# A hybrid SSD and retention decoder layer: three short per-head vectors loaded as rows and spread over the partitions by a matmul

## Chip, cores and metric

The kernel runs on one core of one Trainium2 chip. The metric is the device time of one execution in microseconds (us).

## The reference

One decoder layer on x (1 x 1024 x 1024, float32). RMSNorm, one combined input projection, and its columns go to two groups of heads that are computed side by side: a Mamba-2 state-space group (SSD: 16 heads, chunks of 128 tokens) and a retention group (8 heads). Their outputs are concatenated, projected and added to x; a SwiGLU feed-forward block and a final RMSNorm follow. Three vectors of 16 numbers, one number for each SSD head, matter here:

```python
dt = softplus(dt_raw + dt_bias)                     # dt_bias: 16
a = -exp(a_log)                                     # a_log:   16
a_cs = cumsum(dt * a)                               # within a chunk
...
y = y_diag + y_off + x_c * d_skip[head]             # d_skip:  16
```

## The kernel before

Tokens are worked on in two halves of 512 (h = 0, 1), each of four tiles of 128 tokens. Every float32 matmul of a projection is made of three matmuls on operands split into a rounded part and a rest: `divide(k)` of a block takes one 128-row slice of weights (tile `wr`, 256 KB, five buffers), ScalarE writes the rounded part (line 248) and VectorE the rest (line 249). Below, `wr` slices are counted from 0. A global list of steps, one for each slice of each block, fixes the order on TensorE; `advance` issues weight loads up to three steps ahead of the divided one on SyncE's queue (line 238), and functions hung on a step with `at` run behind it.

The start is written out by hand. SyncE's queue gets the first token tile of x (512 KB), weight slices 0 to 3, the second tile of x, and then slice 4 and on. ScalarE's queue gets the 128x128 identity (`kc`) and `norm1_w`. GpSimd's queue gets the other norm and convolution vectors as rows (`rows`, line 105), which TensorE later turns into columns (`make_cols`). Nine matmuls on a tile of ones go first on TensorE. `turn(0)` then transposes the first token tile; for each of its eight 128-column pieces, ScalarE and VectorE write the split, scaled `h` (lines 1171, 1172), with the weights' divides between them. The first block (`v0`) walks its steps by token tile: steps 0 and 1 are token tile 0, steps 2 and 3 token tile 1, and so on; each step is 12 matmuls of 512 columns. Behind `turn(0)` stand the loads of token tiles 2 and 3, and `load_small()`.

`load_small` issues the load of the large table `kcB` on SyncE and four loads on GpSimd's queue. Two of them fill `dcol` (128 x 8): the lower 64 partitions get the 8 even entries of `d_skip` each, the upper 64 the 8 odd ones, so source and destination pieces are single float32 numbers, two apart in memory. The other two spread `dt_bias` and `a_log` over all 128 partitions of `hb` (128 x 32), 64 bytes to each. Behind step 12 `use_small` turns `a_log` into -exp(a_log) in place (ScalarE line 115, VectorE line 116), and the second `make_cols` does the `rows` (TensorE line 135, ScalarE line 137). `hb` is first read in `dt_stage` of the first half, `dcol` when SSD pieces are put together (line 661).

PSUM has two rings of banks, L (5) for the blocks and M (3) for the rest.

Of the kernel before, what the change touches and what calls it, by code (L numbers as in the profile page):

```python
# [12 lines left out]
AF = mybir.ActivationFunctionType  # L13
# [4 lines left out]
P = 128  # L18
# [6 lines left out]
SH, SP_, SG = 16, 64, 2  # L25
# [40 lines left out]
def block_kernel(ctx: ExitStack, tc: tile.TileContext, x, norm1_w, w_in, conv_w, conv_b,  # L66
                 dt_bias, a_log, d_skip, ssd_norm_w, ret_norm_w, w_out, norm2_w, w_gate,
                 w_up, w_down, final_norm_w, consts, out):
    nc = tc.nc
# [9 lines left out]
    def T(shape, tag, dt=F32, bufs=1):  # L79
        uid[0] += 1  # L80
        return sb.tile(list(shape), dt, tag=tag, name=f"{tag}_{uid[0]}", bufs=bufs)

    def bank(tag):
        uid[0] += 1
        return psum.tile([P, 512], F32, tag=tag, name=f"{tag}_{uid[0]}", bufs={"L": 5, "M": 3}[tag])
# [5 lines left out]
    act = nc.scalar.activation  # L91
# [17 lines left out]
    hb = T([P, 2 * SH], "hb")  # L109
    dcol = T([P, 8], "dcol")  # L110
    ones = T([P, P], "ones")
    nc.vector.memset(ones, 1.0)

    def use_small():
        act(hb[:, SH:2 * SH], hb[:, SH:2 * SH], AF.Exp)
        ts(hb[:, SH:2 * SH], hb[:, SH:2 * SH], -1.0, None, op0=ALU.mult)

    def load_small():
        nc.sync.dma_start(kc, consts[:, P:])
        for j in range(2):  # L120
            nc.gpsimd.dma_start(dcol[64 * j:64 * j + 64, :],
                                d_skip[0].rearrange("(k j) -> j k", j=2)[j]
                                .partition_broadcast(64))
        for j, src in enumerate((dt_bias, a_log)):
            nc.gpsimd.dma_start(hb[:, j * SH:(j + 1) * SH], src[0].partition_broadcast(P))

    dtb = hb[:, 0:SH]
    aneg = hb[:, SH:2 * SH]
# [30 lines left out]
    def mm(o, a, b, start=True, stop=True, **kw):  # L159
        tc.keep_in_program_order(nc.tensor.matmul(o, a, b, start=start, stop=stop, **kw))  # L160
# [1018 lines left out]
    b = bank("M")  # L1179
# [10 lines left out]
    for t in (2, 3):  # L1190
        first_load(t)
    load_small()
    at(ROWS, first_rows)

    def late_small():

        with tc.issue_after(newest["act"]), tc.issue_after(newest["dve"]):
            use_small()
            make_cols(False)
# [78 lines left out]
```

## Time and profile before

| | |
|---|---|
| median of 3 runs (lowest, highest) | 1528.23 us (1526.89, 1529.42) |
| profiled execution, its own time | 1528.46 us |
| its span, first to last instruction | 1526.7 us |
| TensorE matmul busy | 1496.4 us, 98% of the span |
| VectorE, ScalarE, GpSimd busy | 1018.6, 625.2, 33.2 us |
| DMA moved | 208.68 MB |

The span is the time from the first to the last instruction; 1.8 us of the execution's own time lie outside it. Busy shares are averages over the span. Engines are PE (TensorE matmul), PEld (its weight load), DVE (VectorE), ACT (ScalarE), POOL (GpSimd), SP (SyncE); a q behind a name is the engine's queue of DMA issues. An arrow `out<-in` names the tiles, and L248 is line 248 of the kernel.

### The profile page before, as it was taken

What the parts mean: (1) busy time and instruction counts of PE and PEld (TensorE: products, weight loads), DVE (VectorE), ACT (ScalarE), POOL (GpSimd) and SP (SyncE); (2) the same over time, 40 slices, a digit from 0 to 9 for tenths busy, and PEclk for the clock granted to TensorE, in tenths of its full rate; (3) what the DMA queues carried; (4) which work ended last, traced back from release to release, by engine and by line L of the source; (5) the groups of instructions that cost most, each with busy time, mean ns of one, the idle gap of its engine ahead of it and who ended that gap; (6) DMA issues with size and microseconds to landing.
All of it is one profiled execution on the core that took longest, in us unless ns stands there. A gap on an engine that the chain in (4) does not pass through costs nothing.

```text
span 1526.7 us, 20790 instructions
## 1 busy us (share of the span) xinstructions
PE 1496.4 (98%) x7408; PEld 1222.3 (80%) x7408; DVE 1018.6 (67%) x2175; ACT 625.2 (41%) x1219; POOL 33.2 (2%) x67
## 2 busy tenths in 40 slices
PE   6999999999999999999999899999999999999997
PEld 5888878887889878878887688888888887788886
DVE  4587788767688896578746976666666665346345
ACT  5344457444354655333444522222222234344232
POOL 1011000000000000000000000000000000000000
PEclk8999999999999999999999999999999999999999
DMA  7433466473425567645533332222222238455331
GB/s 195 137 92 98 116 203 190 121 242 105 130 77 148 167 204 248 214 146 175 187 118 97 97 111 78 81 83 83 76 83 83 83 105 293 133 176 188 126 112 68
DMA packets 139369, 208.68 MB, mean 137 GB/s; under 512 B 11172, under 2 KB 69376, under 8 KB 139264
## 3 DMA queue, kind: packets, MB, share of 16 engines
q1 hardware_dynamic: 138096, 205.90, 43.6%
q0 software_dynamic: 432, 0.59, 0.6%
q8 instruction: 58, 0.95, 0.3%
q10 hardware_dynamic: 736, 0.86, 0.2%
q14 instruction: 47, 0.39, 0.1%
HBM read 166.34 MB, written 40.96 MB: 136 GB/s over the span
## 4 chain that ended last, share of the span: by engine, by line
PE 92%; DMA 4%; DVE 2%; ACT 1%; issue 1%; SPq 0%; ACTq 0%; DVEq 0%
PE L L160 74%; PE M L160 16%; PE M L163 2%; DMA m<-aD 1%; DMA wr<-in_w_in_dram 1%; DMA wr<-in_w_down_dram 1%; DVE m L196 0%; DMA x<-in_w_gate_dram 0%; DMA kc<-in_consts_dram 0%; DMA ktok<-aD 0%; ACT m L195 0%; DMA m<-mixD 0%; DVE wp L249 0%; DVE u L1019 0%; ACT wp L248 0%
## 5 line engine op out<-in xcount | busy, mean ns | idle before, releaser
L249 DVE TENSOR_TENSOR wp<-wr,wp 128x512 fp32r<-128x512 f32 (+2 forms) x328 | 217.7, 665 | 224.3 <-ACT wp L248 223.1
L160 PE MATMUL L<-wp,m 128*128 128x512 f32 x1512 | 357.3, 395 | 1.5 <-DVE wp L249 0.9
L248 ACT ACTIVATE wp<-wr 128x512 fp32r<-128x512 f32 (+2 forms) x328 | 199.6, 610 | 361.8 <-PE L L160 294.9
L160 PEld LDWEIGHTS L<-wp,m 128*128 128x128 f32 x1512 | 282.0, 188 | 68.7 <-DVE wp L249 2.4
L160 PE MATMUL L<-wp,h 128*128 128x512 f32 (+2 forms) x1248 | 260.0, 365 | 0.0
L160 PEld LDWEIGHTS L<-wp,h 128*128 128x128 f32 x1248 | 215.4, 188 | 30.6 <-issue 5.1
L160 PE MATMUL L<-h,wp 128*128 128x512 f32 x972 | 234.1, 398 | 0.7 <-ACT ktok L166 0.7
L160 PEld LDWEIGHTS L<-h,wp 128*128 128x128 f32 x972 | 180.6, 188 | 44.5 <-ACT ktok L166 1.1
L160 PE MATMUL L<-m,x 128*128 128x512 f32 x336 | 82.7, 395 | 1.6 <-ACT x L195 1.2
L160 PE MATMUL L<-h,x 128*128 128x512 f32 x336 | 83.3, 396 | 0.7 <-ACT ktok L166 0.7
L160 PE MATMUL L<-m,wp 128*128 128x512 f32 x312 | 77.1, 395 | 0.0
L160 PEld LDWEIGHTS L<-m,x 128*128 128x128 f32 x336 | 62.9, 188 | 17.2 <-ACT x L195 1.6
L160 PEld LDWEIGHTS L<-h,x 128*128 128x128 f32 x336 | 62.9, 188 | 16.3 <-ACT ktok L166 1.1
L160 PEld LDWEIGHTS L<-m,wp 128*128 128x128 f32 x312 | 58.5, 187 | 14.4
L195 ACT ACTIVATE wp<-wr 128x512 fp32r<-128x512 f32 x46 | 29.0, 630 | 66.6 <-DVE wr L948 57.5
L195 ACT ACTIVATE x<-x 128x512 fp32r<-128x512 f32 x40 | 24.9, 623 | 72.5 <-PE M L160 32.4
L389 DVE SCALAR_TENSOR_TENSOR m<-m,cols,m 128x512 f32<-128x512 f32 x72 | 52.1, 745 | 3.6 <-ACT m L387 3.4
L160 PE MATMUL M<-m,wp 128*128 128x512 f32 x216 | 53.4, 395 | 0.0
L160 PEld LDWEIGHTS M<-m,wp 128*128 128x128 f32 x216 | 40.5, 188 | 9.9
L160 PE MATMUL M<-m,x 128*128 128x512 f32 x192 | 47.1, 394 | 0.0
L196 DVE TENSOR_TENSOR m<-m 128x512 fp32r<-128x512 f32 x32 | 21.8, 690 | 35.5 <-ACT m L195 35.5
L160 PE MATMUL M<-h,x 128*128 128x512 f32 x180 | 44.5, 395 | 0.0
(280 smaller groups left out, 1952.4 us busy)
## 6 DMA issues: line engine op xcount, KB each, us to landing
wr<-in_w_in_dram SPq DMA_DIRECT2D x144, 256.0 KB, 2.8
wr<-in_w_down_dram SPq DMA_DIRECT2D x88, 256.0 KB, 2.9
wr<-in_w_out_dram SPq DMA_DIRECT2D x64, 256.0 KB, 2.9
aD<-u SPq DMA_DIRECT2D x44, 256.0 KB, 2.0
x<-in_w_gate_dram SPq DMA_DIRECT2D x22, 512.0 KB, 3.9
x<-in_w_up_dram SPq DMA_DIRECT2D x22, 512.0 KB, 3.9
x<-in_x_dram SPq DMA_DIRECT2D x16, 512.0 KB, 4.1
m<-rD SPq DMA_DIRECT2D x16, 512.0 KB, 4.1
```

The lines of the kernel that those rows point to most:

```text
L160: tc.keep_in_program_order(nc.tensor.matmul(o, a, b, start=start, stop=stop, **kw))
L163: tc.keep_in_program_order(nc.tensor.transpose(o, a, ident))
L195: a = act(pair[:, 0], src, AF.Copy).ins
L196: d = tt(pair[:, 1], src, pair[:, 0].bitcast(F32), op=ALU.subtract).ins
L248: newest["act"] = act(pair[:, 0, :n], raw[:, :n], AF.Copy).ins
L249: newest["dve"] = tt(pair[:, 1, :n], raw[:, :n], pair[:, 0, :n].bitcast(F32), op=ALU.subtract).ins
L389: stt(dst, u[:, q:q + TH], w[q], dst, op0=ALU.mult, op1=ALU.add)
```

## The change

The three vectors are loaded as rows of 64 bytes into one partition (a tile of 1 x 48 that shares the buffer `at` with a later tile), from GpSimd's queue right behind the `rows` loads. Behind step 12 one matmul of a row of ones (128 wide) against this row puts all 48 numbers into all 128 partitions of an M bank, and ScalarE copies them from there: `dt_bias` as it is, `a_log` through Exp, and `d_skip` twice, its even entries to the lower 64 partitions of `dcol` and the odd ones to the upper 64. The four spreading loads go.

```diff
+    small = T([1, 3 * SH], "at")
+    for j, src in enumerate((dt_bias, a_log, d_skip)):
+        nc.gpsimd.dma_start(small[:, j * SH:(j + 1) * SH], src)
+
     def use_small():
-        act(hb[:, SH:2 * SH], hb[:, SH:2 * SH], AF.Exp)
+
+        b = bank("M")
+        mm(b[:, :3 * SH], ones[:1, :], small)
+        act(hb[:, :SH], b[:, :SH], AF.Copy)
+        act(hb[:, SH:2 * SH], b[:, SH:2 * SH], AF.Exp)
         ts(hb[:, SH:2 * SH], hb[:, SH:2 * SH], -1.0, None, op0=ALU.mult)
+        d = b[:, 2 * SH:3 * SH].rearrange("p (k j) -> p j k", j=2)
+        for j in range(2):
+            act(dcol[64 * j:64 * j + 64, :], d[64 * j:64 * j + 64, j, :], AF.Copy)
 
     def load_small():
         nc.sync.dma_start(kc, consts[:, P:])
-        for j in range(2):
-            nc.gpsimd.dma_start(dcol[64 * j:64 * j + 64, :],
-                                d_skip[0].rearrange("(k j) -> j k", j=2)[j]
-                                .partition_broadcast(64))
-        for j, src in enumerate((dt_bias, a_log)):
-            nc.gpsimd.dma_start(hb[:, j * SH:(j + 1) * SH], src[0].partition_broadcast(P))
```

## Rows read from the trace of the kernel before

**Rows 1.** The page: busy times, and the span in 40 slices (tenths).

```profile
PE 1496.4 (98%) x7408; PEld 1222.3 (80%) x7408; DVE 1018.6 (67%) x2175; ACT 625.2 (41%) x1219; POOL 33.2 (2%) x67
...
PE   6999999999999999999999899999999999999997
```

**Rows 2.** The chain that ended last, 0 to 120 us: start, us, what.

```profile
0.74 4.60 DMA kc<-in_consts_dram
...
5.36 14.11 DMA wr<-in_w_in_dram
...
19.50 0.63 ACT m L248
...
23.79 6.41 PE L L160 x24
```

**Rows 3.** Waits, 0 to 30 us: total, times, longest.

```profile
PE L L160 <- ACT h L1171: 10.1, 2, 9.9
ACT m L248 <- DMA wr<-in_w_in_dram: 10.0, 1, 10.0
```

**Rows 4.** Timeline of SyncE's queue: start, duration of the issue.

```profile
7.38 0.33 SPq L238 DMA_DIRECT2D wr<-in_w_in_dram  x1
...
8.24 3.73 SPq L238 DMA_DIRECT2D wr<-in_w_in_dram  x1
...
12.06 2.91 SPq L238 DMA_DIRECT2D wr<-in_w_in_dram  x1
...
15.06 1.62 SPq L238 DMA_DIRECT2D wr<-in_w_in_dram  x1
...
16.73 0.62 SPq L1134 DMA_DIRECT2D x<-in_x_dram  x1
```

**Rows 5.** DMA by queue, 0 to 7.8 us.

```profile
DMA packets 1114, 2.01 MB, mean 258 GB/s; under 512 B 209, under 2 KB 395, under 8 KB 1114
...
q0 software_dynamic: 155, 0.04, 2.5%
```

**Rows 6.** DMA by queue, 7.8 to 16.8 us.

```profile
DMA packets 197, 0.33 MB, mean 37 GB/s; under 512 B 81, under 2 KB 89, under 8 KB 197
...
q0 software_dynamic: 68, 0.01, 80.8%
```

**Rows 7.** DMA by queue, 16.8 to 30 us.

```profile
q0 software_dynamic: 65, 0.01, 0.5%
```

**Rows 8.** DMA issues of the first 20 us: KB, median us from issue to landing.

```profile
dcol<-in_d_skip_dram POOLq DMA_DIRECT2D x2, 2.0 KB, 11.6
...
hb<-in_dt_bias_dram POOLq DMA_DIRECT2D x1, 8.0 KB, 13.7
```

**Rows 9.** DMA issues from 60 to 1520 us, the same columns.

```profile
wr<-in_w_in_dram SPq DMA_DIRECT2D x129, 256.0 KB, 2.7
```

**Rows 10.** By stretch: busy times, granted clock, DMA share, GB/s.

```profile
6.00:7.50 1.50, 1.42 (x10) 0.96 (x9) 0.84 (x2) 1.50 (x5) 0.66 (x2) 1.00 1.07 393
...
12.00:19.50 7.50, 0.00 (x0) 0.00 (x0) 0.00 (x0) 0.00 (x1) 0.00 (x0) 0.50 0.84 125
19.50:25.70 6.20, 5.27 (x17) 4.37 (x18) 4.24 (x10) 5.46 (x16) 0.00 (x0) 0.50 0.95 342
25.70:30.20 4.50, 4.50 (x22) 3.69 (x21) 2.36 (x7) 4.02 (x14) 0.00 (x0) 1.00 0.79 265
```

**Rows 11.** Timeline of TensorE, 8 to 58 us.

```profile
8.34 2.15 PE L160 MATMUL L<-m,h 128*128 128x512 f32 x6 [0.17 <-ACT h L1171]
...
21.88 1.91 PE L163 MATMUL M<-kc,x 128*128 128x128 f32 x8
23.44 6.76 PE L160 MATMUL L<-m,h 128*128 128x512 f32 x24
30.04 1.03 PE L163 MATMUL M<-kc,x 128*128 128x128 f32 x8
30.82 5.72 PE L160 MATMUL L<-m,h 128*128 128x512 f32 x24
...
53.03 0.24 PE L135 MATMUL M<-kc,rows 84*128 84x84 f32 x1
```

**Rows 12.** Timeline of ScalarE and VectorE, 7 to 54 us.

```profile
7.53 1.28 DVE L249 TENSOR_TENSOR m<-wr,m 128x512 fp32r<-128x512 f32 x2
...
8.79 0.68 ACT L1171 ACTIVATE h<-M,cols 128x128 fp32r<-128x128 f32 x2
...
28.83 0.35 DVE L1172 SCALAR_TENSOR_TENSOR h<-M,cols,h 128x128 fp32r<-128x128 f32 x1 [0.52 <-ACT h L1171]
...
52.04 0.20 ACT L115 ACTIVATE hb<-hb 128x16 f32<-128x16 f32 x1
...
53.23 0.43 ACT L248 ACTIVATE wp<-wr 128x272 fp32r<-128x272 f32 x1 [0.98 <-PE L L160]
```

## The prediction

> **What bounds the kernel now.** I read the page first: TensorE is busy 98% of the span, and its digit is 9 in nearly every slice but the first, which has a 6 [rows 1]. So a change pays only where TensorE stands still or where it adds to TensorE's own queue, and the first slice is the one place near this change. The chain of work that ended last says what stands in that slice: one weight load, issued at 5.36 us, carries 14.11 us of the chain, and behind it the chain is matmuls nearly without a break [rows 2]. The waits of the first 30 us give the same gap from two sides: ScalarE's divide waits 10.0 us in one piece for a weight slice, and TensorE waits 9.9 us in one piece for the `h` that ScalarE writes behind that divide [rows 3]. ScalarE had ended its work before it at 8.79 + 0.68 = 9.47 us [rows 12] and began the divide at 19.50.
>
> Why does 256 KB take 14 us, when the same load takes 2.7 us later in the kernel [rows 9]? It isn't late issue: slice 4 went out at 5.36 [rows 2], and on SyncE's queue slice 5 at 7.38, in 0.33 us. The issues behind them swell to 3.73, 2.91 and 1.62 us [rows 4]: they are held back by engines that take nothing. The DMA view by queue shows by what. From 7.8 to 16.8 us only 0.33 MB moved, 37 GB/s, where 393 GB/s was reached just before [rows 6, 10]. In those 9 us the software queue, GpSimd's, moved 0.01 MB in 68 packets and held 80.8% of all 16 DMA engines: 0.808 x 9.0 x 16 = 116 us of engine time [rows 6]. The software loads in flight then are those of `dcol` and `hb`, which land 11.6 and 13.7 us after issue [rows 8]. Of the two I blame `dcol`: 2 x 64 x 8 = 1024 separate 4-byte numbers, 116 us / 1024 = 113 ns each. In the stretch behind, 65 software packets take 0.005 x 13.2 x 16 = 1.1 us together, 16 ns each [rows 7], so packets in whole 64-byte or longer pieces are cheap. The sum doesn't hang on this split, since all four loads go.
>
> **The change part by part.**
>
> *Four spreading loads removed.* The 116 us of engine time go, 7.3 us on each of the 16 engines. What is late next? At 7.8 us, 2.01 MB had moved [rows 5], of about 2.1 MB asked for ahead of slice 4 (two token tiles of 0.52 MB, four slices of 0.26 MB, the identity). The rest and slice 4 itself are some 0.4 MB, 1.0 us at 393 GB/s: the last byte passes at about 8.8 us. Landing adds something; 2.7 us from issue to landing, less 0.7 us of transfer, bounds it by 2.0 us [rows 9]. So slice 4 lands between 8.8 and 10.8 us. ScalarE isn't free before 9.47. I take a divide at 9.7 in place of 19.50, nearer the early end, since its descriptors wait ready and part of that 2.0 us is issue: 9.8 us off, bounds 8.6 and 10.0.
>
> Do the next slices keep up? Slice 5, issued at 7.38, lands at about 7.38 + 2.7 = 10.1; slice 6, issued at 8.24, at 10.9; slice 7 waits for its buffer until VectorE ends at 7.53 + 1.28 = 8.81 and lands at about 11.5 [rows 4, 9, 12]. ScalarE asks for them one divide and one `h` piece apart, about 0.77 us: 10.5, 11.25 and 12.0. Each is in time by 0.3 to 0.5 us. The third tile of x, out at 16.73 [rows 4], can go at about 10 and is wanted by transposes at 30.04 - 9.8 = 20.2 [rows 11]. Hence nothing of the 9.8 us is given back there.
>
> *TensorE's clock.* It was granted 0.50 (1.2 GHz) in 12.0 to 19.5 and 19.5 to 25.7 us, and 1.00 (2.4 GHz) from then on [rows 10]; before it fell the engine had stood still since 8.34 + 2.15 = 10.5 us [rows 11]. With the gap down to a few tenths I expect 1.00 throughout. Eight transposes took 1.91 us at the low level and 1.03 at the high, 24 matmuls 6.76 against 5.72 [rows 11]: at most 0.88 + 1.04 = 1.9 us. At least nothing, because the `h` pieces of token tile 1 end at 28.83 + 0.35 = 29.2 us [rows 12], only 1.0 us before the matmuls that use them end, so TensorE can't run far ahead. ScalarE itself would shift some tenths, because its first piece of that tile waits for these transposes. I take 0.8.
>
> The Trainium skill, TensorE: Matmul & The Clock Gate, section HAM oscillation, says that a wait for a DMA makes the gate throttle the array and that the matmuls behind it start cold. The trace agrees (0.50 behind the 9.9 us wait). By it the 0.8 us are earned when the wait goes; without it they are not, and the sum would be 1519.1.
>
> *Three row loads added.* Each is one run of 64 bytes. At the cheap end they cost 16 ns a packet [rows 7]. At the dear end, 113 ns for each of 48 numbers all on one engine, 5.4 us; were `hb` and not `dcol` the culprit, 116 us / 256 runs = 0.45 us a run, 1.4 us for three. I take nothing: the run is contiguous, nearest to the cheap rows. They are issued on GpSimd's queue behind the `rows` loads, where nothing else waits but the memset of `halo`, which is read much later.
>
> *Matmul and copies behind step 12.* TensorE gains one matmul of 48 columns; the nearest row is the 84-column one beside it, 0.24 us [rows 11]. Between 0.1 and 0.5, I take 0.3; it is on the path. ScalarE gains three copies of about 0.20 us [rows 12], and its Exp, which ran free at 52.04, now waits for that matmul, with the next divide queued behind it. That divide stood idle 0.98 us for a buffer before it began [rows 12], since ScalarE works ahead of TensorE there: the three copies and the wait hide in it. Without that cover they would cost some 0.8 + 0.6 us once. The M ring is claimed once more; its banks were read out long before.
>
> *Sum*, against the profiled execution's own 1528.46 us (0.2 above the median shown): 1528.46 - 9.8 - 0.8 + 0.3 = 1518.2.
>
> **The rivals.**
>
> *The clock falls all the same.* While token tile 0 is worked on, ScalarE sets the pace and TensorE runs in pieces; the clock fell at 12.0 us behind just that stage. If it falls at that time again and stays low for the 6 us or more that it was low under work [rows 10], it meets some 3 us of matmuls that ran at full clock before, and these take 1.5 us more at half: instead of 0.8 won, 1.5 lost, 1518.2 + 0.8 + 1.5 = 1520.5. Against it: before, a stop of 10 us stood there.
>
> *Loads come just too late.* The slices pace ScalarE because fixed landing times, hidden before by the long stop, now show: slice 4 at 10.8, and some tenths for each of the next. Then 7.5 us are won and the time is 1520.5 to 1521. Against it: the margins worked out above.
>
> *Rows read number by number on one engine.* 5.4 us on one engine, and every weight slice needs all 16: 1518.2 + 5.4 = 1523.6. Against it: runs of 64 bytes were cheap.
>
> *The stop isn't the small loads'.* The loads removed are 20 KB. If the engines were waiting for something else (memory, or the depth of SyncE's own ring), slice 4 stays late: 1528.46 + 0.3 = 1528.8, no change. Against it: 80.8% of the engines held by that queue alone. The Trainium skill, DMA: Bandwidth & Descriptors, section Anatomy of one DMA, prices such a load at a fixed 2 us plus its bytes, which would make the four loads harmless; the trace disagrees (11.6 us to land, and the engines held).
>
> *Slower.* At step 12 ScalarE holds the next divides while it waits for the new matmul, and TensorE starves. TensorE has three slices in hand there, 12 matmuls of 272 columns each, some 1.5 us a slice; ScalarE would have to stand for 4.6 us plus the 10 us won plus 3 us. Its waits there are 1 us long, and the row loads will have landed 20 us before. Time if so: from 1531.6.
>
> **How the numbers follow.** Two executions of this kernel differ by about 0.1 to 0.2%, so 0.2% (3.1 us) is the bound of what counts as a change. Forecast 0.62; clock 0.14; late loads 0.10; number by number 0.05; not the small loads 0.05; slower 0.04. The forecast's own bounds are 1528.46 - 10.0 - 1.9 + 0.1 = 1516.7 and 1528.46 - 8.6 + 0.5 = 1520.4. The range takes these in, and the clock and the late loads with them, with half a microsecond and more for the spread between executions: 1516.0 to 1521.5. Faster 0.62 + 0.14 + 0.10 + 0.05 = 0.91, same 0.05, slower 0.04.
>
> **What would show it.** Right: ScalarE's wait for a weight slice falls from 10.0 us to under 1; the issues of slices 6 to 8 take about 0.3 to 0.4 us each; the software queue's share from 7.8 to 16.8 us falls from 80.8% to about nothing; the granted clock shows no 0.50 between 12 and 26 us; line 135's neighbour has a new matmul of 0.1 to 0.5 us, and TensorE has no gap there. Wrong: a wait of several us for `wr` or `h` within the first 20 us; a new wait of TensorE for line 248 around 43 us; a software packet share that stays.

## The result, and the profile after

| | before | after |
|---|---|---|
| median (lowest, highest) | 1528.23 us (1526.89, 1529.42), 5 runs | 1518.08 us (1515.91, 1520.32), 5 runs |
| profiled execution, its span | 1528.46, 1526.7 us | 1517.93, 1516.1 us |

The ratio is 0.9935, 95% interval 0.9922 to 0.9949: 0.5 to 0.8% faster. The forecast was 1518.2. The sum came out, but two of its terms were off in opposite directions, so the profile is worth reading term by term.

The page first: its TensorE busy line and the line of slices. The 6 in the first slice is a 9 now [rows 1].

```profile
PE 1494.7 (99%) x7410; PEld 1221.5 (81%) x7410; DVE 1018.2 (67%) x2175; ACT 625.8 (41%) x1222; POOL 36.6 (2%) x66
...
PE   9999999999999999999999899999999999999997
```

The chain of the changed kernel to 120 us (start, us, what), and below it its waits of the first 30 us (total, times, longest):

```profile
4.92 5.64 DMA wr<-in_w_in_dram
...
10.59 0.63 ACT m L253
...
11.52 1.23 PE L L165 x3
12.75 0.87 PE M L168 x8
13.63 5.47 PE L L165 x24
```

```profile
PE L L165 <- ACT h L1176: 1.7, 2, 0.9
...
ACT m L253 <- DMA wr<-in_w_in_dram: 1.5, 2, 1.0
```

The same slice 4 stands on the chain with 5.64 us in place of 14.11, its divide begins at 10.59 in place of 19.50 [rows 2], and the waits of 10.0 and 9.9 us are 1.5 and 1.7 in total [rows 3]. The issues on SyncE's queue no longer swell: the timeline has the five issues of slices 4 to 8 in 5.21 us, 0.33 us each with pauses between them, and the next tile of x at 10.19 in place of 16.73 [rows 4]:

```profile
4.92 5.21 SPq L243 DMA_DIRECT2D wr<-in_w_in_dram  x5
...
10.19 0.42 SPq L1139 DMA_DIRECT2D x<-in_x_dram  x1
```

The DMA view by queue for 7.8 to 16.8 us, the stretch of [rows 6]: 2.79 MB moved where it was 0.33, and the software queue held 0.7% of the engines where it held 80.8%. The second fence is the view of 0 to 7.8 us: the three row loads land 5 to 6 us after issue (KB, us to landing).

```profile
DMA packets 1344, 2.79 MB, mean 310 GB/s; under 512 B 248, under 2 KB 506, under 8 KB 1344
...
q0 software_dynamic: 107, 0.00, 0.7%
```

```profile
at<-in_dt_bias_dram POOLq DMA_DIRECT2D x1, 0.1 KB, 5.9
at<-in_a_log_dram POOLq DMA_DIRECT2D x1, 0.1 KB, 5.6
at<-in_d_skip_dram POOLq DMA_DIRECT2D x1, 0.1 KB, 5.3
```

By stretch, the granted clock (third from the end) stays 1.00 where it was 0.50 [rows 10]:

```profile
12.00:13.50 1.50, 1.50 (x12) 1.18 (x11) 1.42 (x5) 1.50 (x5) 0.00 (x0) 1.00 0.75 263
...
19.50:25.70 6.20, 6.20 (x33) 5.20 (x32) 4.89 (x23) 4.29 (x16) 0.00 (x0) 1.00 0.81 261
```

TensorE's timeline answers to [rows 11]. The first two lines are the transposes and matmuls that took 1.91 and 6.76 us before; the line of `at` is the new matmul.

```profile
12.59 1.03 PE L168 MATMUL M<-kc,x 128*128 128x128 f32 x8
...
13.38 5.72 PE L165 MATMUL L<-m,h 128*128 128x512 f32 x24
...
19.73 5.71 PE L165 MATMUL L<-m,h 128*128 128x512 f32 x24
...
34.34 7.76 PE L165 MATMUL L<-wp,h 128*128 128x272 f32 x60
...
42.02 0.42 PE L165 MATMUL M<-at,ones 1*128 1x48 f32 x2
...
45.58 1.05 PE L165 MATMUL M<-x,ones 128*128 128x128 f32 x8
```

### The profile page after: what moved, and what is told of

Same layout as the page of the kernel before. It is cut to its first block, busy times and chain, and to the rows that moved or that the text cites. A ratio compares the mean times of both kernels' runs of the same rounds, so it can differ in the third digit from the quotient of the medians.

```text
span 1516.1 us, 20797 instructions
## 1 busy us (share of the span) xinstructions
PE 1494.7 (99%) x7410; PEld 1221.5 (81%) x7410; DVE 1018.2 (67%) x2175; ACT 625.8 (41%) x1222; POOL 36.6 (2%) x66
## 4 chain that ended last, share of the span: by engine, by line
PE 94%; DMA 2%; DVE 2%; ACT 1%; issue 1%; SPq 0%; ACTq 0%
PE L L165 76%; PE M L165 17%; PE M L168 2%; DMA m<-aD 1%; DMA wr<-in_w_down_dram 0%; DVE m L201 0%; DMA wr<-in_w_in_dram 0%; DMA m<-mixD 0%; DMA kc<-in_consts_dram 0%; DVE wp L254 0%; ACT wp L253 0%; ACT m L200 0%; ACT u L205 0%; DVE M L892 0%; ACT x L451 0%
```

## The experiments

Theory A, from the prediction: the two loads of `dcol` hold the DMA engines, at a price for each single 4-byte number. Rivals: all four spreading loads hold them alike (B); what counts is the spreading over partitions, not the size of the pieces (A2); or the place beside the first loads makes them slow. All spans below are of one profiled execution, and a kernel without a median or a ratio ran once. Executions of the kernel before lie between 1525.6 and 1530.4 us in all, so the readings rest on the rows more than on the times. Software time is the software queue's share of a stretch, times 16 engines, times its length: 7.8 to 16.8 us unless another is named.

| kernel | time, us | span, us | software time, us | ScalarE's wait for slices |
|---|---|---|---|---|
| before | 1528.46 | 1526.7 | 116 | 10.0 |
| changed | 1517.93 | 1516.1 | 1.0 | 1.5 |
| d_skip alone by row | 1521.41 | 1519.6 | 17 | 2.3 |
| dt_bias, a_log alone by row | 1526.48 | 1524.7 | 106 | 9.7 |
| dcol in 32-byte runs | 1517.71 | 1515.9 | 24 | 2.2 |
| half of dcol in runs | 1525.97 | 1524.2 | 58 | 5.4 |
| dcol loaded twice | 1537.08 | 1535.3 | 230 (7.8 to 28.8 us) | 19.3 |
| gaps in the tile, none in memory | 1527.43 | 1525.7 | 116 | 9.6 |
| dcol only moved to step 24 | 1528.90 (median of 10: 1527.26) | 1527.1 | 112 | 10.7 |
| dcol held back to step 24 | 1519.10 (median of 5: 1520.44) | 1517.3 | 115 (72 to 84 us) | 1.9 |

**One half of the change at a time.** The first kernel sends only `d_skip` through row and matmul, the second only the other two vectors.

```diff
-        for j in range(2):
-            nc.gpsimd.dma_start(dcol[64 * j:64 * j + 64, :], ...)
...
+    small = T([1, SH], "at")
+    nc.gpsimd.dma_start(small, d_skip)
...
```

> Only d_skip goes through the row and the matmul; dt_bias and a_log are spread by DMA as in the kernel before. Theory A (the 1024 single 4-byte numbers of dcol hold the DMA engines): the whole gain, a span of 1516 to 1518 us, ScalarE's wait for weight slice 4 under 2 us, and the software queue's share from 7.8 to 16.8 us at a few per cent. Theory B (all four spreading loads hold them, hb by its 256 pieces as much as dcol): a share of that queue of 30% or more and a span of 1520 to 1523 us. Theory C (the stop is not the small loads', and the changed kernel only starts otherwise): no telling, a span anywhere from 1516 to 1527 us without relation to that queue's share.

> Only dt_bias and a_log go through the row and the matmul; dcol is loaded as in the kernel before. Theory A: nothing is won, a span of 1526 to 1528 us, a wait of ScalarE for weight slice 4 of 9 to 10 us, a share of the software queue near 80% from 7.8 to 16.8 us, and the clock at 0.50 behind 12 us. Theory B: part of the gain, 1520 to 1523 us.

Software queue of the first and of the second kernel, 7.8 to 16.8 us:

```profile
q0 software_dynamic: 106, 0.02, 12.1%
```

```profile
q0 software_dynamic: 127, 0.01, 73.8%
```

`d_skip` is the culprit: with its loads left, the share stays at 73.8% and ScalarE's waits for slices at 9.7 us in total; with them gone the two are 12.1% and 2.3 us. But neither span lies in the range that theory A gave.

The first kernel's, 1519.6 us, lies between the ranges of A and B, 3.5 us above the changed kernel's. (Its time is 8.7 us less than that of the kernel before that ran beside it, 1530.07.) The software queue, with `hb` alone to spread, cost some 17 us of engine time here, which theory A had at next to nothing. TensorE stood still for 2.21 us, where it does for 0.93 us in the changed kernel, and the clock fell behind it. By stretch, then TensorE's timeline:

```profile
12.30:15.60 3.30, 3.15 (x12) 2.71 (x12) 2.64 (x6) 2.79 (x8) 0.00 (x0) 0.50 0.97 309
```

```profile
12.45 1.65 PE L164 MATMUL L<-m,h 128*128 128x512 f32 x3 [2.21 <-ACT h L1175]
13.90 1.90 PE L167 MATMUL M<-kc,x 128*128 128x128 f32 x8
```

The eight transposes take 1.90 us at 0.50, as in the kernel before, with the slow loads gone. At the second block TensorE is 2.2 us behind the changed kernel (36.53 against 34.34 us); where the other 1.3 us of the 3.5 come from is open.

The second kernel's span, 1524.7 us, is 1.3 us under theory A's range. Its 9.7 us are three waits, not the one of 9 to 10 us expected:

```profile
ACT m L253 <- DMA wr<-in_w_in_dram: 9.7, 3, 4.6
```

The loads of `dcol` went out from 5.11 us here, just behind the issue of slice 4 (4.96), and from 4.09 us in the kernel before, ahead of it (5.36). That this order split the wait and won the 2 us is argued, not shown. So B is refuted as a theory of equal shares, but it isn't quite empty.

**The size of the pieces.** Same bytes, same partitions, eight neighbouring numbers in place of every second one.

```diff
-            nc.gpsimd.dma_start(dcol[64 * j:64 * j + 64, :],
-                                d_skip[0].rearrange("(k j) -> j k", j=2)[j]
-                                .partition_broadcast(64))
+            nc.gpsimd.dma_start(dcol[64 * j:64 * j + 64, :],
+                                d_skip[0, 8 * j:8 * j + 8].partition_broadcast(64))
```

> The kernel before, with dcol loaded from 8 neighbouring numbers of d_skip in place of every second one: the same bytes to the same partitions, but as 128 pieces of 32 bytes. The heads' skips are mixed up by it; the work is the same. Theory A in its narrow form (it is the number of pieces, 1024 against 128): the stop goes, a span of 1516 to 1517 us (no matmul is added), the software queue's share under 10%. Rival A2 (it is the spreading of 2 KB over 128 partitions, whatever the pieces): the stop stays, 1526 to 1528 us.

The span is 1515.9 us, and the software queue's line for 7.8 to 16.8 us is

```profile
q0 software_dynamic: 139, 0.02, 16.7%
```

The stop went without a matmul, so A2 falls. The share is above the 10% expected, again with `hb` spread early.

> The kernel before, with the lower half of dcol loaded as before (512 single numbers) and the upper half from 8 neighbouring numbers (64 pieces of 32 bytes); the skips of the upper half are mixed up by it. Theory A with a price for each number: the software queue holds about 58 us of engine time (half of 116), weight slice 4 lands 3 to 5 us late in place of 9, and the span is 1520 to 1523 us. If one such load is enough to stop the engines for as long as two, 1526 to 1528 us; if two are needed to fill the rings, 1516 to 1518 us.

> The kernel before, with the two strided loads of dcol issued a second time into a tile that nothing reads (2048 single numbers in place of 1024). Theory A with a price for each number: about 230 us of engine time, the divide of slice 4 (or of the next slices) some 7 us later, span 1532 to 1535 us. Rival (a fixed length of the stop, or loads that overlap): 1526 to 1529.

Half of `dcol` in runs, 7.8 to 16.8 us, then the doubled loads, 7.8 to 28.8 us:

```profile
q0 software_dynamic: 139, 0.02, 40.3%
```

```profile
q0 software_dynamic: 195, 0.03, 68.4%
```

512, 1024 and 2048 numbers hold the engines for 58, 116 and 230 us: 113, 114 and 112 ns a number (with what little the queue carries besides; 106 us, 104 ns, in the kernel with `dt_bias` and `a_log` by row). The price goes with the count. The waits follow: 5.4, 10.0 and, in three pieces, 19.3 us. The span of the doubled kernel is 0.3 us beyond the range expected; that of the half kernel, 1524.2, is 1.2 us above its range, although its wait fell as theory A has it. Its clock also fell behind the stop, to 0.50 from 14 to 20 us.

The last variant reads eight neighbours and writes them two apart, into a tile of 128 x 8 x 2.

```diff
-    dcol = T([P, 8], "dcol")
+    dcol = T([P, 8, 2], "dcol")[:, :, 0]
... (the loads as with the 32-byte runs)
```

> The kernel before, with 8 neighbouring numbers of d_skip read for each partition but written two apart in the tile, so the pieces are single numbers for the writing side alone (the skips of the heads are mixed up by it). If the price is that of 4-byte pieces: engine time 100 us or more, span 1525 to 1528. If it is that of gaps in the memory read: under 30 us, span 1515 to 1518.

Its software queue, 7.8 to 16.8 us:

```profile
q0 software_dynamic: 77, 0.01, 80.5%
```

The full price again. In the kernel before only the memory read has gaps (`dcol` is 128 x 8 without any); here only the tile has. A gap on either side costs as much as the other, which fits single numbers as the pieces.

**The place.** The first kernel only has the two loads behind step 24 in the program.

> The kernel before, with the two strided loads of dcol issued behind step 24, many steps ahead of their first use, and nothing through TensorE; hb is spread at the start as before. Theory A (single numbers hold the engines wherever they stand): the software queue holds them for 100 us or more again, at 80 to 110 us of the span; the weights are two to three steps ahead (5 to 8 us), so at most 1 to 4 us of a stop come back there: span 1517 to 1522. Rival (they are slow only at the start, beside the first loads): under 20 us of engine time, no stop, span 1517 to 1519.

It tests nothing of the place. Nothing on GpSimd's queue held the loads, and they went out at 5.2 us, right behind those of `hb`; software share 77.5%, time 1527.26 us, ratio 0.9997 (0.9987 to 1.0006). The second puts a GpSimd copy that writes `dcol` in front of them, whose source is ready only near 70 us:

```diff
+    def load_dcol():
+        nc.gpsimd.tensor_copy(dcol, halo[:, 6:9, :].rearrange("p c q -> p (c q)")[:, :8])
+        ... (the two loads)
+    at(24, load_dcol)
```

> The kernel before, with the two strided loads of dcol held back to step 24: a GpSimd copy that writes dcol from the halo of the second convolution block goes before them, so they can't be issued before some 80 us. hb is spread at the start as before, nothing goes through TensorE. Theory A (single numbers hold the engines wherever they stand): the software queue holds them for 90 us or more then, 5 to 7 us of each engine; the weights are two to three steps ahead, so 0 to 4 us of a stop come back there and the span is 1516 to 1521. Rival (slow only at the start, beside the first loads): under 20 us of engine time there, span 1516 to 1518.

The loads were issued at 71 us. Software queue, 72 to 84 us, and below it the waits of that kernel from 84 to 92 us:

```profile
q0 software_dynamic: 64, 0.00, 59.8%
```

```profile
ACT wp L251 <- DMA wr<-in_w_in_dram: 2.0, 1, 2.0
...
PE L L163 <- ACT x L520: 0.5, 1, 0.5
```

0.598 x 12 x 16 = 115 us: the price is the same 60 us later, with no first loads beside it. What changes is who pays. Weights are divided ahead by then, so 7 us of held engines become one wait of 2.0 us on ScalarE and 0.5 us on TensorE. The ratio is 0.9959 (0.9944 to 0.9973), against 0.9935 for the change: more than half of the gain, from the place alone.

**The clock.** To part the clock from the loads, 40 useless matmuls of ones fill the stop of the kernel before.

```diff
+                    if self.first == 0 and k == 0 and kk == 3:
+                        for _ in range(FILL):
+                            mm(self.ps[3][:, :P], ones, ones)
```

> The kernel before with its slow loads, and 40 added matmuls of ones (128 columns, some 0.22 us each) on TensorE where it stands still, ahead of the last three matmuls of step 0: about 8.7 us of useless work inside the stop of 9.9 us. Theory (the stop costs its own length and, through the clock, the matmuls behind it 2.2 us more): the granted clock stays 1.00 past 12 us, ScalarE's divide of slice 4 stays at 19 to 20 us, and from that divide to the first matmul of the second block it takes 23.7 us as in the changed kernel in place of 25.9; span 1524 to 1525 us. Rival (those 2.2 us were other things, the loads coming sooner): still 25.9 us, span 1526 to 1528.

> The stop of the kernel before filled with 40 useless matmuls of ones again, now written to an L bank that has no other use before step 6, so that they claim no M bank. Theory (a standing TensorE loses the clock, which costs 2.2 us behind the stop): granted clock 1.00 from 12 to 26 us; from ScalarE's divide of slice 4 to the first matmul of the second block 23.7 us, as in the changed kernel, in place of 25.9 us; span 1524 to 1525 us. Rival (the 2.2 us came from the loads and not from the clock): still 25.9 us and 1526 to 1528 us.

In the first of the two (into an M bank) half of the next transposes waited 1.82 us for VectorE's `h` pieces, which read the M banks, in the second they did not; both came out slower than before, 1532.10 and 1535.42 us, which neither theory had. In the second, by stretch, then TensorE's and ScalarE's timelines:

```profile
12.00:19.50 7.50, 7.50 (x69) 7.44 (x67) 0.00 (x0) 0.51 (x1) 0.00 (x0) 1.00 0.89 142
19.50:25.70 6.20, 4.99 (x25) 3.51 (x23) 3.63 (x8) 6.20 (x20) 0.00 (x0) 1.00 0.93 336
```

```profile
19.93 1.23 PE L160 MATMUL L<-m,h 128*128 128x512 f32 x3 [0.29 <-ACT h L1174]
21.00 1.03 PE L163 MATMUL M<-kc,x 128*128 128x128 f32 x8
...
28.37 0.73 PE L160 MATMUL L<-m,h 128*128 128x512 f32 x2 [3.59 <-ACT h L1174]
```

```profile
21.85 0.62 ACT L200 ACTIVATE u<-x 128x512 f32<-128x512 f32 x1
...
27.97 0.61 ACT L1174 ACTIVATE h<-M,cols 128x128 fp32r<-128x128 f32 x2
```

The slow loads are all there (ScalarE's divide of slice 4 at 18.99 us) and the clock stays at 1.00; the three matmuls behind the stop and the eight transposes take 1.23 and 1.03 us, as in the changed kernel. With `d_skip` alone by row it was the other way round: the slow loads gone, a stop of 2.21 us left, and 1.65 and 1.90 us at 0.50. So it is the standing engine that lost the clock, not the loads. But the added matmuls also changed the order of ScalarE's list: squares of x (line 200) now stand ahead of the `h` pieces, and TensorE waits 3.59 us for one, which is some of the time lost. The price of the clock for the whole stage could not be read off this kernel.

**Without the matmul.** All three vectors are spread from SyncE's queue in runs of 64 bytes, behind the large table; GpSimd picks the even and odd entries.

```diff
+        for j in range(2):
+            nc.gpsimd.tensor_copy(dcol[64 * j:64 * j + 64, :], d[64 * j:64 * j + 64, j, :])
...
+        for j, src in enumerate((dt_bias, a_log, d_skip)):
+            nc.sync.dma_start(hb[:, j * SH:(j + 1) * SH], src[0].partition_broadcast(P))
```

> No matmul and no software loads: dt_bias, a_log and d_skip are spread over 128 partitions in runs of 64 bytes from SyncE's queue behind the large table, and GpSimd copies the even and odd entries of d_skip into dcol at step 12. If the new matmul's 0.5 us on TensorE is all that is left to win, the span is 0.5 us under the changed kernel's and the times can't be told apart; if 384 runs of 64 bytes hold up the loads behind them on SyncE's queue, TensorE stops again at 20 to 35 us and it is 1 to 3 us slower than the changed kernel.

> The changed kernel once more, on the same chip as the three above: a span of 1514 to 1518 us, with ScalarE's divide of slice 4 at 10 to 11 us and the first matmul of the second block at 34 to 35 us.

1516.89 us (1516.05 to 1518.00) without the matmul and 1517.72 us (1516.05 to 1519.05) for the changed kernel once more; ratios to the kernel before 0.9927 (0.9915 to 0.9940) and 0.9932 (0.9920 to 0.9945). The times don't part the two. TensorE's timeline of the kernel without the matmul does, in its own stage:

```profile
34.31 7.76 PE L159 MATMUL L<-wp,h 128*128 128x272 f32 x60
...
45.06 1.05 PE L159 MATMUL M<-x,ones 128*128 128x128 f32 x8
```

The 384 runs of 64 bytes cost TensorE nothing here: the second block begins at 34.31 us, against 34.34 in the changed kernel.

## Why the prediction was right, step by step

*What holds the engines* was right in every part that it named: the loads of `dcol`, by single numbers. The price predicted, 113 ns a number, held at three counts and at another place. At equal bytes, the loads landed 11.6 us after issue as single numbers [rows 8] and 5.0 us after it in 32-byte runs. The rival by a fixed cost of a load, taken from the Trainium skill's DMA: Bandwidth & Descriptors, section Anatomy of one DMA, falls with that: the cost of these loads goes with the number of their pieces at equal bytes.

*The stop*: 9.8 us forecast (8.6 to 10.0), 8.9 measured (19.50 to 10.59). The step that was mis-sized is the landing of slice 4, taken at about 9.7 us; it landed at 4.92 + 5.64 = 10.56, near the late end of the bounds. In this stage the weight loads took a median of 5.0 us from issue to landing, against the 2.7 us from later in the kernel [rows 9] that the bounds were made of. Slice 2 cost ScalarE the other 0.5 us of the 1.5. The sign named for this, a wait of ScalarE under 1 us, was missed by that much.

*The clock*: 0.8 us forecast, at most 1.9; 2.2 measured. The lead of the changed kernel is 8.9 us at the divide and 30.82 - 19.73 = 11.1 us at the second group of 24 matmuls [rows 11]. The chain of the kernel before has

```profile
20.43 1.65 PE L L160 x3
22.08 1.71 PE M L163 x8
```

and 6.41 us for the 24 matmuls behind them [rows 2]; against 1.23, 0.87 and 5.47 us in the chain above, that is 0.42 + 0.84 + 0.94 = 2.2 us. (A chain counts no time twice, so its pieces are shorter than the same work in a timeline.) Two steps failed. The bound counted transposes and 24 matmuls and left out the three matmuls ahead of them, which also ran at the low level. And the cap by the `h` pieces of token tile 1 did not hold: those pieces came sooner as well, ending at 18.96 + 0.35 = 19.3 us, 9.9 us before their old time. The cap was misread, too: by the order of the steps, the 24 matmuls that end at 30.2 us are steps 1 and 2, and half of those pieces are first read by step 3, from 30.82 us on.

That the stop took the clock with it is shown by the filled stop, and with it some 1.3 us of the 2.2, for the three matmuls and the transposes. That the 0.94 us of the 24 matmuls are the clock's as well is argued from the rows at either level, not shown.

The rival by which the clock falls all the same did not come true in the changed kernel, and it did with `d_skip` alone by row. Its price was too low by its own terms: 3 us of matmuls at half the clock take 3 us more, not 1.5, which gives 1522.0 us, outside the range.

*The matmul*: 0.3 us forecast (0.1 to 0.5), 0.5 measured. From the first matmul of the second block to the eight matmuls of ones against `x` (they spread the row norms over the partitions), TensorE takes 45.58 - 34.34 = 11.24 us with it and 45.06 - 34.31 = 10.75 without; in the kernel before, 56.18 - 45.43 = 10.75. The nearest row, a single transpose, was too small: this matmul is two records, 0.42 us.

*The row loads* at nothing: right. *The copies on ScalarE* hidden: right. In the timeline of ScalarE the four copies stand between two divides that each still waited for TensorE (idle time in brackets):

```profile
42.13 0.43 ACT L253 ACTIVATE wp<-wr 128x272 fp32r<-128x272 f32 x1 [1.09 <-PE L L165]
...
42.62 0.35 ACT L127 ACTIVATE dcol<-M 64x8 f32<-64x8 f32 x2
...
44.26 0.64 ACT L253 ACTIVATE wp<-wr 128x512 fp32r<-128x512 f32 x1 [0.91 <-PE L L165]
```

Together 8.9 + 2.2 - 0.5 = 10.6 us. That is the lead at those eight matmuls of ones (56.18 - 45.58), where the change has had its effect, and also the difference of the two spans (1526.7 - 1516.1). That the spans repeat it to a tenth is luck: on the way the lead changes by more than a microsecond. At the start of the feed-forward block it is 8.7 us (the chain before, then after):

```profile
862.41 2.60 PE L L160 x10
```

```profile
853.72 2.59 PE L L165 x10
```

Single executions of the changed kernel differ by more (spans from 1514.1 to 1518.5 us). Two misses of about a microsecond, one each way, made the sum look better than its terms.

## What to carry to other kernels

A DMA of 2 KB can be the largest transfer of a stage: count its pieces, not its bytes, and look at the share of the engines beside the MB of each queue. Where a short vector must be spread, give the DMA whole runs (from SyncE's queue, 384 of 64 bytes cost TensorE nothing here) and pick the entries apart on an engine, or hold the load back to where the loads that others wait for are far ahead; the route through the matmul was no faster than runs of 64 bytes with two small copies. At a stop of TensorE, price the matmuls behind it too, all of them, and don't cap the gain by a neighbour that moves forward with it.

## What was not expected

The spreading of `hb`, 256 runs of 64 bytes, took next to nothing when it stood behind the slow loads [rows 7]. Where GpSimd's queue had it alone to spread at the start, the share from 7.8 to 16.8 us was 12.1% with `d_skip` alone by row and, with `dcol` held back,

```profile
q0 software_dynamic: 70, 0.02, 15.5%
```

That is 17 and 22 us; less the 1.0 us that this queue takes in the changed kernel, an estimated 16 to 21 us of engine time. Going first is not the whole reason: with `dcol` only moved to step 24, `hb` went first as well, and the two together took 112 us, no more than the 116 us of the kernel before. Why is open.

No run sends the single numbers from another queue. Whether the 113 ns are the price of such pieces on any queue or on GpSimd's alone is open, too.

Where the feed-forward block begins, the clock fell for 3.4 us in the profiled execution of the changed kernel and not in that of the kernel before, with TensorE equally idle ahead of it. In the second profiled execution of the changed kernel it fell there as well (0.53 from 842.6 to 846.0 us). Why is open. By stretch, the changed kernel, then the kernel before:

```profile
838.00:843.60 5.60, 3.34 (x18) 2.58 (x18) 5.54 (x10) 4.04 (x7) 0.00 (x0) 1.00 0.01 3
843.60:847.00 3.40, 3.40 (x11) 2.72 (x10) 3.40 (x6) 1.75 (x3) 0.00 (x0) 0.50 0.60 176
```

```profile
848.00:853.60 5.60, 3.34 (x19) 2.66 (x18) 5.54 (x9) 3.83 (x7) 0.00 (x0) 1.00 0.00 0
853.60:857.00 3.40, 2.71 (x12) 1.88 (x10) 3.40 (x7) 2.35 (x5) 0.00 (x0) 1.00 0.76 218
```
